# Sixteen sums of the convolution taps, from VectorE's adds to accumulating transfers on GpSimd's queue

## The chip, the core and the metric

The kernel runs on one core of a Trainium2 chip. TensorE multiplies matrices into PSUM, VectorE and ScalarE do the elementwise work, GpSimd does a little elementwise work and issues DMA transfers on its own queue, and SyncE issues the weight loads. The metric is the time of one execution in device microseconds; lower is better.

## The reference

One decoder layer with two token mixers in parallel, latent attention and a short gated convolution. The part that matters here is the convolution over 256 tokens and 2048 channels, with three taps:

```python
u = c_gate * c_in
u_pad = jnp.pad(u, ((0, 0), (CONV_K - 1, 0), (0, 0)))
conv = sum(conv_w[k] * u_pad[:, k:k + s] for k in range(CONV_K))
y_conv = jnp.einsum('bse,ed->bsd', b_gate * conv * jax.nn.silu(z_conv), w_o_conv)
```

For each token the result is `conv_w[2]*u[s] + conv_w[1]*u[s-1] + conv_w[0]*u[s-2]`. Around it stand the input projections (`h @ w_in`), the attention with 16 heads, the gates, and the output projections, all in float32.

## The kernel before

**Weights.** All weights come from HBM in units of 128 x 2048 numbers (1 MB), loaded by SyncE into three `raw` buffers. Each unit is split in two halves of 1024 columns. ScalarE copies a half to `whi` (the leading part of each number, line 245), and VectorE subtracts to get the rest, `wlo` (line 246). There are five buffers of each. A product of two such split matrices takes three matmuls. For one unit TensorE runs 24 matmuls, over two row blocks of 128 tokens (`t` = 0 and 1), and both halves are read in both row blocks. Every matmul is pinned in program order, and all have line 88.

**Heads and column blocks.** The middle of the kernel is a loop over 16 heads, `h = 4*v + at`. Beside the attention of head `h`, four units of `channels(h, i)` compute 512 columns of one of the four convolution projections. So four heads make one column block `j` of 512 channels: `u = c_gate * c_in` at `at` = 1, the gate `b_gate` at 2, `z_conv` at 3. `u` of block `j` and row block `t` is the tile `cv_f[:, j, t]` (128 tokens x 512 channels); the product of the gates is `cv_w[:, t]`.

**The taps.** `taps(j, t)` is a generator with three steps, resumed by hand with `next(tap)` between pieces of the attention:

- Step one. On GpSimd's queue, `u` is copied to two tiles shifted by one and two tokens (`mv1x`, `mv2x` in the code, `mv` in the profile, one buffer each); the first rows come from the earlier row block or from a memset. The rows of the convolution's weights for these taps are fetched, broadcast to 128 partitions (`cw`, two buffers).
- Step two. VectorE multiplies both shifted copies by their weights and adds the second to the first (line 785). The third tap's weights are fetched into a `cw` buffer that the first product has released.
- Step three. VectorE multiplies `u` by the third tap's weights and adds the sum of the other two to it (line 785).

After that `channels_join(j, t)` multiplies `u` by the gates (line 756), transposes it in 32 x 32 blocks into `cw` (t = 1) or `mv2x` (t = 0) on VectorE (line 320), and GpSimd's queue writes it to DRAM in four pieces (line 328, `far`) and brings it back turned (line 332). The joined blocks are split into `cv_both` (ScalarE and VectorE) in the next stage, at the second and third groups of projections.

For row block 1 the second step runs at `at` = 2 and the third at the end of that head, the join one head later. For row block 0 step one runs at the end of `at` = 3, steps two and three in the first four units of the next block's first head, and the join two units later. The last column block has no next block: its row block 0 follows directly on row block 1, and steps two and three run inside the last head.

**Order.** What is passed to `keep_in_program_order` is placed on its engine behind everything written before it; all taps, the transfers through DRAM and the softmax's transfers are pinned so. Weight splits, softmax arithmetic, the join's product and its transpose are placed by a planner, which fixes the order of each engine's queue when the kernel is built. An engine works its queue in that order, and a waiting instruction holds what stands behind it. GpSimd's queue carries all the transfers of the taps, of the softmax (`far<-via`, `p<-far`), of the gates (`far<-cw`, `at_f<-far`) and of the joins (`far<-mv`, `cv_f<-far`).

After the head loop the memory of `mv`, `cw` and the other temporaries is given up and used again by `at_both` and `cv_both`.

Of the kernel before, what the change touches and what calls it, by code (L numbers as in the profile page):

```python
# [15 lines left out]
ALU = mybir.AluOpType  # L16
# [66 lines left out]
def tile_layer(ctx: ExitStack, tc: tile.TileContext, xw, w0, xb, x, pos, pvec, post_g, wc, wz, wcv, wkr, wqk, wqr, wv, cwr, wsq, out):  # L83
    nc = tc.nc
# [223 lines left out]
    def temp(name, shape=(P, S), dt=F32, bufs=2, tag=None):  # L308

        tag, n = tag or name.rstrip("0123456789_"), shape[-1]  # L310
        if n % LINE == 0:
            return bp.tile(list(shape), dt, name=name, tag=tag, bufs=bufs)
        return bp.tile([P, -(-n // LINE) * LINE], dt, name=name, tag=tag, bufs=bufs)[:, :n]
# [449 lines left out]
    def taps(j, t):  # L763

        u, parts = cv_t[:, j, t, :], []

        def bring(dst, src):

            tc.keep_in_program_order(nc.gpsimd.dma_start(out=dst, in_=src))

        for d in (1, 2):
            m = temp(f"mv{d}", (P, 512), bufs=1, tag=f"mv{d}x")
            if t:
                bring(m[:d, :], cv_t[P - d :, j, 0, :])
            else:
                tc.keep_in_program_order(nc.gpsimd.memset(m[:d, :], 0.0))
            bring(m[d:, :], u[: P - d, :])
            parts.append(m[:, :])
        def tap(d):
            cw = temp("cw", (P, 512), bufs=2)  # L780
            bring(cw[:, :], cwr[2 - d : 3 - d, 512 * j : 512 * (j + 1)].to_broadcast([P, 512]))
            return cw

        def join(dst, a, b, op):
            tc.keep_in_program_order(nc.vector.tensor_tensor(dst, a, b, op=op))

        cws = [tap(d) for d in (1, 2)]
        yield
        for a, cw in zip(parts, cws):
            join(a, a, cw[:, :], ALU.mult)  # L790
        join(parts[0], parts[0], parts[1], ALU.add)
        cw = tap(0)
        yield
        join(u, u, cw[:, :], ALU.mult)
        join(u, u, parts[0], ALU.add)
        yield

    cv_w = bp.tile([P, NT, 512], F32, name="cv_w")
# [14 lines left out]
    for h in range(H):  # L813
# [88 lines left out]
        if at == 1:  # L902
            tap = taps(v, 1)
            next(tap)
        elif at == 3 and h + 1 < H or h == H - 2:
            tap = taps(v, 0)
            next(tap)
# [286 lines left out]
```

## Time and profile before

| | |
|---|---|
| median of 3 runs | 1035.13 us (1034.82 to 1035.21) |
| span of the profiled execution | 1033.7 us |
| TensorE busy | 1027.6 us, 99% |
| VectorE busy | 683.5 us, 66% |
| ScalarE busy | 527.4 us, 51% |
| GpSimd busy | 178.7 us, 17% |
| moved by DMA | 233.25 MB, 226 GB/s |

The page gives the span of the profiled execution, from its first to its last instruction; its own time is not listed beside it, and the three timed runs lie 1.1 to 1.5 us above the span. In the rows, PE is TensorE, PEld its weight loads, DVE VectorE, ACT ScalarE, POOL GpSimd and SP SyncE; L785 is line 785 of the kernel. A row of a group says how often an operation ran, its shortest, median and longest duration in ns, and the start of the first and the last in us. In a row of a timeline stand the start, the duration, the engine, the line and the operation; the bracket has the idle time before it and what ended it. In a row of DMA issues the last number is the median time from issue to landing.

### The profile page before, as it was taken

How to read it: one execution, taken by the hardware profiler on the slowest of the kernel's cores; microseconds unless marked ns; L12 is line 12 of the kernel's file. 1: busy time of each engine (PE TensorE's matmuls, PEld its weight loads, DVE VectorE, ACT ScalarE, POOL GpSimd, SP SyncE). 2: the span in 40 equal slices, each digit the busy share in tenths (PEclk: the TensorE clock that was granted, in tenths of full speed). 3: DMA queues.
4: the chain of work that ended last, by engine and by line, in shares of the span. 5: the costliest groups of instructions: out<-in, count | busy, mean ns of one | idle time of the engine just before them, and what ended most of it. 6: DMA issues, size and time to landing. Idle time of an engine off the chain costs nothing.

```text
span 1033.7 us, 12740 instructions
## 1 busy us (share of the span) xinstructions
PE 1027.6 (99%) x4684; PEld 856.7 (83%) x4684; DVE 683.5 (66%) x957; ACT 527.4 (51%) x735; POOL 178.7 (17%) x344
## 2 busy tenths in 40 slices
PE   9999999999999999999999999999999999999998
PEld 8888888888888888888888888888888888888886
DVE  7588787787777777777777785564455455455562
ACT  7665545655456454564555565344434444443451
POOL 4540421104300223112133120020010001002000
PEclk9999999999999999999999999999999999999999
DMA  9775865668665676857686765565565557558642
GB/s 353 278 261 204 276 221 219 211 197 288 215 250 193 223 265 209 275 187 242 228 270 226 265 217 199 204 226 185 200 219 209 188 201 241 183 188 337 228 163 81
DMA packets 44526, 233.25 MB, mean 226 GB/s; under 512 B 7952, under 2 KB 10512, under 8 KB 21552
## 3 DMA queue, kind: packets, MB, share of 16 engines
q1 hardware_dynamic: 32400, 199.67, 54.6%
q0 software_dynamic: 11632, 29.48, 8.8%
q10 hardware_dynamic: 432, 3.29, 0.8%
q8 instruction: 36, 0.59, 0.2%
q14 instruction: 26, 0.21, 0.1%
HBM read 215.66 MB, written 12.58 MB: 221 GB/s over the span
## 4 chain that ended last, share of the span: by engine, by line
PE 96%; DMA 2%; ACT 1%; DVE 0%; issue 0%; DVEq 0%; SPq 0%
PE cv L88 34%; PE sq L88 34%; PE out L88 8%; PE z L88 6%; PE qa L88 2%; PE vv L88 2%; PE kn L88 2%; PE qn L88 2%; PE ckv L88 2%; PE sc L88 1%; PE qr L88 1%; PE o L88 1%; DMA raw<-wz_dram 1%; DMA at_f<-far_qa 1%; DMA at_f<-far_ckv 0%
## 5 line engine op out<-in xcount | busy, mean ns | idle before, releaser
L246 DVE TENSOR_TENSOR wlo<-raw,whi 128x1024 fp32r<-128x1024 f32 (+1 forms) x370 | 440.5, 1196 | 279.8 <-ACT whi L245 268.4
L245 ACT ACTIVATE whi<-raw 128x1024 fp32r<-128x1024 f32 (+1 forms) x372 | 382.4, 1035 | 401.6 <-PE sq L88 180.5
L88 PE MATMUL cv<-whi,x_both 128*128 128x512 f32 x1024 | 319.8, 389 | 0.0
L88 PEld LDWEIGHTS cv<-whi,x_both 128*128 128x128 f32 x1024 | 192.3, 188 | 39.4
L88 PE MATMUL cv<-wlo,x_both 128*128 128x512 f32 x512 | 199.6, 390 | 0.0
L88 PE MATMUL sq<-whi,x_both 128*128 128x512 f32 x512 | 158.3, 389 | 0.0
L88 PEld LDWEIGHTS sq<-whi,x_both 128*128 128x128 f32 x512 | 96.1, 188 | 19.9
L88 PEld LDWEIGHTS cv<-wlo,x_both 128*128 128x128 f32 x512 | 96.1, 188 | 19.5 <-DVE wlo L246 0.2
L88 PE MATMUL sq<-wlo,x_both 128*128 128x512 f32 x256 | 99.6, 389 | 0.0
L88 PE MATMUL z<-whi,x_both 128*128 128x512 f32 x256 | 80.0, 389 | 0.0
L88 PE MATMUL sq<-whi,at_both 128*128 128x512 f32 x256 | 79.5, 389 | 0.0
L88 PE MATMUL sq<-whi,cv_both 128*128 128x512 f32 x256 | 79.5, 389 | 0.0
L88 PE MATMUL out<-whi,m_both 128*128 128x512 f32 x256 | 78.9, 389 | 0.0
L328 POOL DMA_DIRECT2D far<-sg x32 | 17.5, 553 | 313.0 <-DVE sg L320 238.4
L328 POOL DMA_DIRECT2D far<-via x64 | 35.1, 556 | 177.9 <-DVE via L320 177.9
L88 PEld LDWEIGHTS sq<-wlo,x_both 128*128 128x128 f32 x256 | 48.0, 188 | 10.0
L88 PEld LDWEIGHTS sq<-whi,at_both 128*128 128x128 f32 x256 | 48.0, 188 | 9.9
L88 PEld LDWEIGHTS out<-whi,m_both 128*128 128x128 f32 x256 | 48.0, 188 | 9.9
L88 PEld LDWEIGHTS sq<-whi,cv_both 128*128 128x128 f32 x256 | 48.0, 188 | 9.9
L88 PEld LDWEIGHTS z<-whi,x_both 128*128 128x128 f32 x256 | 48.1, 188 | 9.9
L88 PE MATMUL z<-wlo,x_both 128*128 128x512 f32 x128 | 49.8, 389 | 0.0
L88 PE MATMUL sq<-wlo,at_both 128*128 128x512 f32 x128 | 49.8, 389 | 0.0
(216 smaller groups left out, 1128.9 us busy)
## 6 DMA issues: line engine op xcount, KB each, us to landing
raw<-wsq_dram SPq DMA_DIRECT2D x80, 1024.0 KB, 4.8
raw<-wcv_dram SPq DMA_DIRECT2D x64, 1024.0 KB, 5.6
raw<-wz_dram SPq DMA_DIRECT2D x16, 1024.0 KB, 4.9
raw<-wqk_dram SPq DMA_DIRECT2D x8, 1024.0 KB, 6.0
cw<-cwr_dram POOLq DMA_DIRECT2D x24, 256.0 KB, 6.0
raw<-wc_dram SPq DMA_DIRECT2D x4, 1024.0 KB, 10.5
raw<-wv_dram SPq DMA_DIRECT2D x4, 1024.0 KB, 4.8
far<-via POOLq DMA_DIRECT2D x64, 48.0 KB, 4.1
```

Source lines behind the costliest of these rows:

```text
L88: return tc.keep_in_program_order(nc.tensor.matmul(*a, **kw))
L245: a = nc.scalar.activation(hi, src, AF.Copy)
L246: b = nc.vector.tensor_tensor(lo, src, hi.bitcast(F32), op=ALU.subtract)
L328: tc.keep_in_program_order(queue.dma_start(out=f[i], in_=m))
```

## The change

Both adds of `taps` become DMA transfers with an accumulating write: GpSimd's queue sends the one tile onto the other, and the transfer adds it. The first adds the second shifted product to the first; the second adds their sum to `u`. `taps` runs eight times (four column blocks, two row blocks), so sixteen adds of 128 x 512 float32 are replaced. The products stay on VectorE. The new transfers are pinned in program order on GpSimd's queue, the first ahead of the fetch of the third tap's weights.

```diff
+        def summed(dst, src):
+            tc.keep_in_program_order(nc.gpsimd.dma_start(out=dst, in_=src, accum_op=ALU.add))
+
         cws = [tap(d) for d in (1, 2)]
         yield
         for a, cw in zip(parts, cws):
             join(a, a, cw[:, :], ALU.mult)
-        join(parts[0], parts[0], parts[1], ALU.add)
+        summed(parts[0], parts[1])
         cw = tap(0)
         yield
         join(u, u, cw[:, :], ALU.mult)
-        join(u, u, parts[0], ALU.add)
+        summed(u, parts[0])
         yield
```

## The prediction

> **What bounds the kernel now.** I read the page first (busy shares, chain), then what TensorE waited for, then the chain in order of time. A row is start, duration and work, with the idle time before it in brackets.
>
> ```profile
> span 1033.7 us, 12740 instructions
> PE 1027.6 (99%) x4684; PEld 856.7 (83%) x4684; DVE 683.5 (66%) x957; ACT 527.4 (51%) x735; POOL 178.7 (17%) x344
> PE 96%; DMA 2%; ACT 1%; DVE 0%; issue 0%; DVEq 0%; SPq 0%
> ```
>
> The page's chain says that TensorE's own work makes up 96% of it. Its waits (us in total, times, longest), all rows that the view has for it, and then two pieces of the chain in order of time:
>
> ```profile
> PE idle L88 <- PEq L1182: 0.8, 1, 0.8
> PE fin L88 <- ACT dg L1069: 0.4, 1, 0.4
> PE vv L88 <- DVE f L396: 0.2, 1, 0.2
> 210.46 5.44 PE vv L88 x24
> 222.63 16.32 PE cv L88 x72
> ```
>
> TensorE is the bound. In the whole span it waited 1.4 us that the waits view can name (0.8 + 0.4 + 0.2), and only the 0.2 us was a wait for VectorE. The 72 matmuls in 16.32 us are three weight units of 24, so one unit of matmuls lasts 5.44 us. The matmul order is written out by hand, and the change leaves it alone. So the question is not what the sums cost VectorE, but whether a sum that lands later ever holds up a weight half that TensorE needs.
>
> Next, how busy the engines are where sums stand (the windows view: us, then TensorE, weight loads, VectorE, ScalarE, GpSimd, granted clock, DMA share, GB/s), and how far ahead of TensorE the splits work (timelines of ScalarE and VectorE).
>
> ```profile
> 210.00:262.00 52.00, 52.00 (x243) 43.48 (x242) 40.34 (x64) 27.43 (x41) 13.69 (x25) 1.00 0.71 240
> 600.16 1.06 ACT L245 ACTIVATE whi<-raw 128x1024 fp32r<-128x1024 f32 x1 [3.03 <-PE sq L88]
> 601.47 1.06 ACT L245 ACTIVATE whi<-raw 128x1024 fp32r<-128x1024 f32 x1 [0.24 <-PE sq L88]
> 601.26 2.53 DVE L246 TENSOR_TENSOR wlo<-raw,whi 128x1024 fp32r<-128x1024 f32 x2 [1.23 <-ACT whi L245]
> ```
>
> In the stretch around one sum VectorE works 40.34 of 52 us (78%), GpSimd 13.69, at a granted clock of 1.00. ScalarE's whi copies wait for TensorE to release one of five buffers: the split engines run at the end of their buffers. From this I estimate the cover. The release behind 600.16 comes when TensorE is through with the first half of its unit, 1.36 us (a quarter of 5.44) before that unit ends. That unit ends near 601.2 and the one after it at 606.6. At the release the buffers hold the other half of that unit, both halves of the next one and the first half of the one behind it; the freed buffer takes that last unit's second half. TensorE reaches it 1.36 us into the unit that starts at 606.6, at 608.0. Its wlo, the first of the two at 601.26, is ready at about 602.5. So VectorE may stand still for about 5.5 us before TensorE waits.
>
> **The change, part by part: what goes.**
>
> ```profile
> L785 DVE TENSOR_TENSOR mv<-mv,mv x8: 680/692/695, 151.3 to 582.3; 128x512 f32<-128x512 f32 x8
> L785 DVE TENSOR_TENSOR cv_f<-cv_f,mv x8: 678/687/693, 175.9 to 594.9; 128x512 f32<-128x512 f32 x8
> ```
>
> VectorE loses 8 x 0.692 + 8 x 0.687 = 11.0 us in sixteen pieces. TensorE's only wait for VectorE is 0.2 us, so this is worth between 0 and 0.2 us. I take 0.
>
> **What comes: sixteen transfers of 256 KB from SBUF to SBUF on GpSimd's queue.** No accumulating transfer is in the trace. Its nearest rows:
>
> ```profile
> L769 POOL DMA_DIRECT2D mv<-cv_f x24: 507/552/560, 138.7 to 573.4; - x24
> mv<-cv_f POOLq DMA_DIRECT2D x8, 254.0 KB, 4.2
> mv<-cv_f POOLq DMA_DIRECT2D x8, 252.0 KB, 5.2
> cw<-cwr_dram POOLq DMA_DIRECT2D x24, 256.0 KB, 6.0
> DMA to landing us min/median/max: 1.5/5.6/7.9
> cv_f<-x_dram SPq DMA_DIRECT2D x1, 2048.0 KB, 10.7
> ```
>
> An issue takes 0.55 us of GpSimd (below: 0.51, the shortest of that row; above, since two inputs are read: twice, 1.1), so 16 x 0.55 = 8.8 us (8.2 to 17.6) on an engine that is busy 17%. The landing, from issue: below 1.5 us, the fastest of line 769; above 10.7 us, the transfer of eight times the bytes. I take 6.0, the slow end of the plain 256 KB rows, because the accumulating one also reads its destination. DMA engines are 0.71 busy in this stretch; the data of sixteen sums, read twice and written once, are 16 x 0.75 = 12 MB, or 12 GB/s over the span beside the 240 of this stretch. I cost that at 0 because the whi copies wait for TensorE, not for weights.
>
> The Trainium skill gives, in "DMA: Bandwidth & Descriptors" (Anatomy of one DMA), a fit of about 2.0 us plus bytes over 436e3 for a DMA from GpSimd: an estimate of 2.6 us here. The plain rows above take 4.2 to 6.0, so the measurement decides; by the page the landing would be earlier and the sum stays 0.
>
> The Trainium skill also has a rule against this change, in "SBUF — State Buffer" (SBUF: two separate sides, the "DVE blocks DMA" trap): while VectorE runs a two-port operation, GpSimd cannot write the descriptors of its transfers. By it issues would stretch beside VectorE. The trace does not agree for these neighbours: 24 issues of line 769 lie between 0.507 and 0.560 us beside a VectorE that is busy most of the time.
>
> **Where the new waits stand.** A column block has a pair of sums for its second row block (t=1) and one for its first (t=0). For t=1, on VectorE, the second sum and its reader:
>
> ```profile
> 175.87 0.69 DVE L785 TENSOR_TENSOR cv_f<-cv_f,mv 128x512 f32<-128x512 f32 x1
> 198.26 0.69 DVE L756 TENSOR_TENSOR cv_f<-cv_f,cv_w 128x512 f32<-128x512 f32 x1
> ```
>
> and for t=0, rows of GpSimd and VectorE in order of time:
>
> ```profile
> 213.84 0.55 POOL L769 DMA_DIRECT2D cw<-cwr_dram  x1 [5.90 <-DVE mv L785]
> 215.37 0.69 DVE L785 TENSOR_TENSOR mv<-mv,mv 128x512 f32<-128x512 f32 x1
> 219.63 0.69 DVE L785 TENSOR_TENSOR cv_f<-cv_f,cw 128x512 f32<-128x512 f32 x1 [0.17 <-DMA cw<-cwr_dram]
> 223.49 1.22 DVE L246 TENSOR_TENSOR wlo<-raw,whi 128x1024 fp32r<-128x1024 f32 x1
> 224.62 0.68 DVE L756 TENSOR_TENSOR cv_f<-cv_f,cv_w 128x512 f32<-128x512 f32 x1
> 232.73 2.21 POOL L328 DMA_DIRECT2D far<-via  x4 [18.34 <-DVE via L320]
> 240.10 0.57 POOL L332 DMA_DIRECT2D p<-far  x1 [5.17 <-ACT whi L245]
> 255.69 2.17 POOL L328 DMA_DIRECT2D far<-mv  x4
> ```
>
> t=1: the second sum would come behind four far<-via issues of the softmax (2.21 us for four, as at 232.73 below), be issued near 178 and land near 184. Its reader, the join with cv_w (line 756), is at 198.3, 14 us later. Even at 10.7 us nothing waits. Cost 0, four times.
>
> t=0, first sum: it waits for both products (215.37), is issued by 215.9, and stands ahead of the tap-0 fetch, which moves from 213.84 to about 215.9, 2.1 us. That fetch would land near 222, so the product that reads it moves from 219.63 to about 222. If VectorE's order still has it ahead of the wlo at 223.49, the queue behind it (softmax sums, V splits, that wlo) stands about 2.4 us. That wlo now ends at 224.7 and is needed 5.44 + 1.36 us after the unit boundary at 222.63, at 229.4: cover 4.7 us. 2.4 is inside it.
>
> t=0, second sum: in GpSimd's program order it comes behind the four far<-via, so it moves from 221.7 on VectorE to an issue at 234.9 and lands near 241. Queued behind it on GpSimd are the softmax's return p<-far, which stands idle until 240.10 anyway, so the 0.55 us issue fits in its 5.17 us gap, and later far<-mv at 255.69, the first that reads the joined block. Join and transpose (0.68 + 0.70) then end near 243: 12 us of room. Cost 0, three times, as long as the join does not stand in VectorE's queue for more than 5.5 us.
>
> **The last block** is the tightest, since the next tap reuses the buffer that the second sum reads:
>
> ```profile
> 570.41 0.68 DVE L785 TENSOR_TENSOR cv_f<-cv_f,cw 128x512 f32<-128x512 f32 x1
> 571.88 0.52 POOL L776 MEMSET mv<- 1x512 f32 x1 [5.59 <-DVE cv_f L785]
> 581.00 1.31 DVE L785 TENSOR_TENSOR mv<-mv,cw 128x512 f32<-128x512 f32 x2 [0.20 <-DMA cw<-cwr_dram]
> 593.38 0.69 DVE L785 TENSOR_TENSOR cv_f<-cv_f,cw 128x512 f32<-128x512 f32 x1
> 597.59 0.68 DVE L756 TENSOR_TENSOR cv_f<-cv_f,cv_w 128x512 f32<-128x512 f32 x1
> 605.06 0.57 POOL L332 DMA_DIRECT2D cv_f<-far  x1 [0.58 <-DMA far<-mv]
> 607.87 4.26 ACT L245 ACTIVATE at_both<-at_f 128x512 fp32r<-128x512 f32 x8
> L88 PE MATMUL sq<-whi,at_both x256: 389/389/389, 633.9 to 916.6; 128*128 128x512 f32 x128
> 644.59 0.61 ACT L245 ACTIVATE cv_both<-cv_f 128x512 fp32r<-128x512 f32 x1
> ```
>
> With 6.0 us: the sum is issued at 571.1, lands at 577.1, so the memset is 5.2 us later and the two products start at 586.2 instead of 581.0. They end at 587.5; the first sum lands at 593.5; the fetch behind it is issued at 588.1 and lands at 594.1; the product runs to 594.8; the second sum lands at 600.8, and the join starts 3.2 us later than 597.59. The return to cv_f moves from 605.06 to about 608 and lands by 614. The split that reads it is at 644.59: 30 us of room. With 10.7 us everywhere the same chain gives a join at about 614 and a landing near 626, still 18 us early. The copies of at_both reuse memory that the last transposed transfer frees, so they move to about 609 (621 with 10.7, done by 626); TensorE first reads them at 633.9, so even this is inside. Sum over all parts: 0 us on TensorE's chain, 0 to 0.2 us gained. The profiled span of 1033.7 lies 1.4 us below the median of 1035.13, and I keep that distance: 1033.7 + 0 + 1.4 = 1035.1.
>
> **The rivals.** *First: the fetch is held by the sum ahead of it, and it is slower.* The tap-0 fetch stands right behind the first sum on one queue. If its data also waits for the sum's, it lands another 4 to 5 us later; with the 2.4 us above the product holds VectorE for 6.4 to 7.4 us against a cover of 4.7. Price 1.7 to 2.7 us in each of three blocks, and about as much again (4 x 1.5 us) where the last block waits at four points behind a landing later than its order expects: 3 x 2.2 + 6 = 12.6 us at most, 1041 in the middle. It decides once the fetch lands more than 8.3 us after its issue (6.0 + 4.7 - 2.4). For it: line 769 already reaches 7.9. Against it: the two mv<-cv_f transfers of a tap are issued close together on that queue and still land in 4.2 and 5.2 us. Chance 0.26.
>
> *Second: the accumulating transfer itself is slow.* Nothing in the trace bounds it firmly. Landing L us after issue against an order made for about 5.2, the t=0 join stands L - 5.2 us in VectorE's queue in four places, weight splits behind it; beyond 5.5 us of cover TensorE waits. It decides at L = 10.7; at 15 us it costs 4 x 4.3 = 17 us: 1052. The Trainium skill, "DMA: Bandwidth & Descriptors" (Rules for kernel authors), says that an accumulate reads its destination and writes it later; no run here shows what that costs. Chance 0.15; with a remainder of 0.02, slower has 0.43.
>
> *Third: a gain.* It needs TensorE to be waiting for VectorE. The waits name 1.4 us in all, the start included; less VectorE work cannot return more than 0.2 us unless the order of the splits falls out better. That also covers sums that turn out free. Time at best 1033. Chance 0.05.
>
> **How the numbers follow.** About 0.2%, 2 us, is what a measurement of this kernel can tell from no change. My forecast, everything hidden, has 0.52 and gives 1035.1. The range goes from 1033.4 (a little below the 0.2 us gain) to 1047 (the first rival's 12.6 us rounded down); it leaves out the second rival's 0.15 and what lies below. Alone, the likeliest case runs from 1034.5 to 1037.
>
> **What would show it.** Right: line 785 keeps 24 products and loses 16 sums, VectorE falls to about 672 us, GpSimd's rows gain sixteen issues near 0.55 us landing near 6, TensorE's waits stay under 2 us. Wrong: a row of TensorE waiting for wlo, near 220, 355, 489 or 585 to 610; VectorE waiting for cw (first rival) or for the sum at line 756 (second). A landing beyond 10.7 us breaks the forecast.

## The result, and the profile after

The changed kernel takes 1041.4 us in the median (1039.77 to 1041.79, three runs) against 1035.13 us: 1.0057 times as long, with a 95% interval of 1.0038 to 1.0077. The forecast of 1035.1 us with everything hidden was wrong; the time lies where the first rival put it, but that is luck, since the reason is another one. The profiled execution took 1039.77 us; its span is 1038.0 us, 4.3 us longer than before, and the two other runs were 1.6 and 2.0 us slower than it. Here and below, runs more than 1.5% above the fastest of their kernel are left out of the ratios; this concerns one run with plain copies and one with the fetches first.

The page of the changed kernel (span, busy time of each engine, shares of the chain), then all rows of TensorE's waits (us in total, times, longest):

```profile
span 1038.0 us, 12762 instructions
PE 1028.7 (99%) x4684; PEld 857.6 (83%) x4684; DVE 671.7 (65%) x941; ACT 528.6 (51%) x735; POOL 195.1 (19%) x360
PE 95%; DMA 2%; DVE 1%; issue 1%; POOL 0%; ACT 0%; DVEq 0%; ACTq 0%; POOLq 0%
PE o L88 <- DVE pt L246: 3.1, 1, 3.1
PE idle L88 <- PEq L1185: 0.8, 1, 0.8
PE fin L88 <- ACT dg L1072: 0.4, 1, 0.4
```

and the two longest rows of VectorE's waits that concern the taps:

```profile
DVE cv_f L756 <- DMA cv_f<-mv: 12.1, 4, 3.6
DVE mv L785 <- DMA cw<-cwr_dram: 9.5, 4, 7.3
```

VectorE lost 11.8 us of work and TensorE gained one wait of 3.1 us, in one place, for VectorE's split of `pt`: the softmax weights of a head, turned, which the `o` matmuls multiply with the values. Of VectorE's own two waits, which the rivals spoke of, the first is new, and the second was 4.1 us before; only a part of them reaches TensorE. Now the transfers: issues by line and tile (ns shortest/median/longest), then landings (us, median).

```profile
L788 POOL DMA_DIRECT2D mv<-mv x8: 896/920/980, 151.4 to 591.3; - x8
L788 POOL DMA_DIRECT2D cv_f<-mv x8: 867/956/974, 177.0 to 598.2; - x8
DMA to landing us min/median/max: 3.9/6.3/9.2
mv<-mv POOLq DMA_DIRECT2D x8, 256.0 KB, 5.5
cv_f<-mv POOLq DMA_DIRECT2D x8, 256.0 KB, 7.2
```

Landings of 5.5 and 7.2 us lie around the predicted 6.0. The first three blocks go as forecast in this execution. For the first block's t=0 (its second and third steps run beside the second block's first head) the rows of GpSimd and VectorE are:

```profile
214.62 0.90 POOL L788 DMA_DIRECT2D mv<-mv  x1 [7.71 <-DVE mv L785]
220.36 0.69 DVE L785 TENSOR_TENSOR cv_f<-cv_f,cw 128x512 f32<-128x512 f32 x1 [0.62 <-DMA cw<-cwr_dram]
231.52 0.97 POOL L788 DMA_DIRECT2D cv_f<-mv  x1
238.74 0.69 DVE L756 TENSOR_TENSOR cv_f<-cv_f,cv_w 128x512 f32<-128x512 f32 x1 [3.59 <-DMA cv_f<-mv]
```

The fetch behind the first sum holds its product for 0.62 us, not for 6. The join stands 3.59 us in VectorE's queue, less than the 5.5 us of cover, and TensorE shows no wait there.

The last block is where the time goes. Rows of VectorE, GpSimd and TensorE in order of time; the row that starts with 578.69 is a piece of the chain of waits, from the issue of the second weight fetch to the start of the product:

```profile
571.02 0.69 DVE L785 TENSOR_TENSOR cv_f<-cv_f,cw 128x512 f32<-128x512 f32 x1 [1.30 <-DMA cw<-cwr_dram]
572.01 0.88 POOL L788 DMA_DIRECT2D cv_f<-mv  x1 [6.81 <-DVE cv_f L785]
576.11 0.52 POOL L776 MEMSET mv<- 1x512 f32 x1 [2.66 <-DMA cv_f<-mv]
578.69 8.64 DMA cw<-cwr_dram
587.33 0.69 DVE L785 TENSOR_TENSOR mv<-mv,cw 128x512 f32<-128x512 f32 x1 [7.30 <-DMA cw<-cwr_dram]
589.07 0.69 DVE L785 TENSOR_TENSOR mv<-mv,cw 128x512 f32<-128x512 f32 x1
...
591.60 0.55 DVE L246 TENSOR_TENSOR pt<-p,pt 128x384 fp32r<-128x384 f32 x1
592.30 0.71 PE L88 MATMUL o<-pt,vv_hi 128*128 128x512 f32 x1 [3.15 <-DVE pt L246]
592.30 1.35 PE o L88 x4
593.65 349.26 PE sq L88 x1536
```

and of before, at the same place (not shown above):

```profile
573.90 1.10 POOL L769 DMA_DIRECT2D cw<-cwr_dram  x2
586.95 0.56 DVE L246 TENSOR_TENSOR pt<-p,pt 128x384 fp32r<-128x384 f32 x1
589.77 0.39 PE L88 MATMUL o<-pt,vv_hi 128*128 128x512 f32 x1
589.93 0.57 PE o L88 x4
590.51 348.20 PE sq L88 x1536
```

Up to here the changed execution runs 0.78 us ahead of the earlier one on TensorE, so rows of before are moved by that much below.

- The first product was late by 587.33 - (581.00 - 0.78) = 7.1 us. The product of `u` starts 571.02 - (570.41 - 0.78) = 1.4 us late, because its fetch stands behind the first sum and lands later. From that start to the memset it took 576.11 - 571.02 = 5.1 us instead of 571.88 - 570.41 = 1.5: 3.6 us for a transfer that landed in 4.05 us where VectorE added in 0.69. From the issue of the second weight fetch to the product it then took 8.64 us instead of 6.55 (before, that fetch was issued near 574.45, the middle of the row of two, and the product began at 581.00): 2.1 us of the 7.1. By their own landings the two fetches took 9.0 and 9.5 us, and 7.0 each before.
- The `pt` split stands in VectorE's queue behind both products, two `wlo` splits and two short operations of the attention. It starts 591.60 - (586.95 - 0.78) = 5.4 us late. Before, it was done at 587.51 for a matmul at 589.77: 2.3 us of cover. 5.4 - 2.3 = 3.1 us, the wait that TensorE shows.
- Then TensorE was slow. The four `o` matmuls and the matmuls of the next stage (`sq`) took 1.35 and 349.26 us; before, 0.57 and 348.20. That is 0.78 + 1.06 = 1.8 us on top of the wait, and the granted clock says why (windows of 1 us; the columns as in the windows row of before):

```profile
591.00:592.00 1.00, 0.00 (x0) 0.00 (x0) 0.97 (x3) 0.00 (x0) 0.70 (x2) 1.00 0.80 328
592.00:593.00 1.00, 0.70 (x2) 0.64 (x3) 0.97 (x3) 0.00 (x0) 0.75 (x2) 0.68 1.04 442
593.00:594.00 1.00, 1.00 (x6) 0.90 (x5) 1.00 (x2) 0.36 (x1) 0.00 (x0) 0.50 0.96 246
```

The clock is 1.00 during the wait, falls to 0.50 when TensorE works again, and comes back within the window of 595 (0.61 in the mean). Sum: -0.78 + 3.15 + 1.8 = 4.2 of the 4.3 us.

### The profile page after: what moved, and what is told of

Its sections match the earlier page's. It is cut to its first block, busy times and chain, and to the rows that moved or that the text cites. A ratio compares the mean times of both kernels' runs of the same rounds, so it can differ in the third digit from the quotient of the medians.

```text
span 1038.0 us, 12762 instructions
## 1 busy us (share of the span) xinstructions
PE 1028.7 (99%) x4684; PEld 857.6 (83%) x4684; DVE 671.7 (65%) x941; ACT 528.6 (51%) x735; POOL 195.1 (19%) x360
## 4 chain that ended last, share of the span: by engine, by line
PE 95%; DMA 2%; DVE 1%; issue 1%; POOL 0%; ACT 0%; DVEq 0%; ACTq 0%; POOLq 0%
PE sq L88 34%; PE cv L88 30%; PE z L88 8%; PE out L88 8%; PE qa L88 2%; PE kn L88 2%; PE qn L88 2%; PE vv L88 2%; PE ckv L88 2%; PE sc L88 1%; PE qr L88 1%; PE o L88 1%; DMA cw<-cwr_dram 1%; DMA mv<-mv 1%; DMA cv_f<-mv 0%
## 5 line engine op out<-in xcount | busy, mean ns | idle before, releaser
L245 ACT ACTIVATE whi<-raw 128x1024 fp32r<-128x1024 f32 (+1 forms) x372 | 382.9, 1035 | 401.1 <-PE sq L88 180.3
```

The costliest lines, as they stand in the source:

```text
L245: a = nc.scalar.activation(hi, src, AF.Copy)
```

## The experiments

Three theories stood against each other. **A**: one place costs, the second sum of the last block's t=1, through the `pt` split; the other fifteen transfers are nearly free. **B**: the loss is many small pieces, spread over all blocks. **C**: the accumulating write itself is slow, and a plain transfer would do no harm. Every kernel was timed beside the kernel before on the same chip; its medians there were 1035.17, 1035.69 and 1035.47 us for the three sets, and all 73 of its runs there had a mean granted clock of 0.999 or 1.000.

### All but the one sum, and only that one

```diff
-        summed(u, parts[0])
+        if (j, t) == (NV - 1, 1):
+            join(u, u, parts[0], ALU.add)
+        else:
+            summed(u, parts[0])
```

> All sums but one are transfers: the second sum of the last block's second row block (u plus the tap sum, near 572 us) is VectorE's add again. Theory A (the loss is one chain: that sum's landing holds the memset of the next tap, its copies and fetches, so the two products start 7 us late in VectorE's queue and the softmax split of head 15 behind them makes TensorE wait): the products start about 3.6 us earlier than in the changed kernel, TensorE's wait for pt falls from 3.1 us to 0 to 0.8 us, and the time is 1035 to 1036. Theory B (fifteen other transfers and issues of 0.9 us on GpSimd's queue, spread over the kernel, cost it): the time stays within 0.5 us of the changed kernel, near 1041.

Measured: 1036.26 us (1035.05 to 1038.64, 11 runs), ratio 1.0009 [1.0001, 1.0018]. Fifteen of sixteen transfers cost 0.1%, 0.3 us more than A's upper end. TensorE's wait for `pt` is gone.

The converse has this one transfer alone, all other sums on VectorE:

> Only that one sum is an accumulating transfer, the other fifteen are VectorE's. Theory A: the products start 3.6 to 5.7 us later than before, less a cover of 2.3 us that pt had, so TensorE waits 1.3 to 3.4 us for pt and, with the lower granted clock after the wait, the time is 1037 to 1040. Theory B: one sixteenth of the loss, 1035 to 1036.

Measured: 1036.48 us (1035.7 to 1040.33, 12 runs), ratio 1.0016 [1.0006, 1.0025]: between the two expectations. The profiled execution, the slowest, has the stall (`8.74` is the landing of the second weight fetch), while seven of the twelve runs lie below 1037:

```profile
PE o L88 <- DVE pt L246: 2.7, 1, 2.7
577.98 8.74 DMA cw<-cwr_dram
```

So the one transfer is enough to make the stall, but alone it does so only in some runs. In the changed kernel the chain starts 1.4 us later, behind the fetch that the first sum holds; here the first sum is an add, and the product of `u` starts without a wait. That this makes the difference is argued from the rows; no run has these two sums alone.

### Block by block

The last block's four sums alone as transfers:

> Only the last column block's four sums are transfers; the twelve of the first three blocks are adds on VectorE. Theory A (one place costs: in the last block the second sum of (3,1) delays the products, and behind them a pt split that TensorE has only 2.3 us of cover for; the other fifteen are nearly free): a wait of TensorE for pt of 2 to 3.5 us near 592, then a low granted clock, 1039 to 1041 us. Theory B (the loss is made of many small pieces in all four blocks): 1036 to 1037.

Measured: 1041.35 us (1037.08 to 1042.12, 6 runs), ratio 1.0047 [1.0031, 1.0063]. As much as the whole loss is in these four. The profiled execution took 1037.78 us and has the wait without the fall of the clock:

```profile
PE o L88 <- DVE pt L246: 2.2, 1, 2.2
```

Four of its six runs took 1041.3 to 1042.1 us at a mean granted clock of 0.996 or 0.997, and two 1037.1 and 1037.8 us at 0.999 and 1.000.

The complement, the twelve of the first three blocks:

> Twelve of the sixteen sums are transfers: those of the first three column blocks. The last block's four are VectorE's. Theory A (the loss comes from the last block alone, where the next tap follows at once and the memory is reused behind it): the time is that of the kernel before, 1035.2 within 0.5 us, and TensorE waits for no split. Theory B (issues and landings anywhere on GpSimd's queue): twelve sixteenths of the 6 us stay, 1039 to 1040.

Measured: 1036.96 us (1035.28 to 1039.91, 11 runs), ratio 1.0014 [1.0005, 1.0022]. Not nothing, as A had it, and not B's 4 us. Two landings of t=0 sums lay on its chain (the two pieces below), so the twelve were parted by row block:

```profile
232.47 7.54 DMA cv_f<-mv
368.31 7.11 DMA cv_f<-mv
```

> Only the t=0 pairs of the first three blocks are transfers (six). The kernel with twelve transfers there showed 1.3 to 1.4 us more than its comparison, and its chain of waits ran through the landing of cv_f<-mv that the t=0 join waits for at line 756 (7.1 to 7.5 us), with wlo splits behind it. If that wait is where those 1.3 us go: 1036.3 to 1037, and TensorE shows a wait of under 1 us. If they lie elsewhere (t=1, or GpSimd's extra issues): 1035.1 to 1035.9.

> Only the t=1 pairs of the first three blocks are transfers (six). Their second sum has 14 us until the join reads it. If the t=0 join is where the first three blocks lose: no difference, 1035.1 to 1035.9. If every transfer costs a little wherever it stands: about half of the 1.3 us, 1035.8 to 1036.5.

Measured: t=0 alone 1036.65 us (1035.15 to 1039.19, 12 runs), ratio 1.0012 [1.0003, 1.0020]; t=1 alone 1035.35 us (1034.54 to 1036.77, 11 runs), ratio 0.9998 [0.9989, 1.0006]. The t=1 transfers of these blocks are free, those of t=0 are not quite. TensorE's new wait in the t=0 kernel, and its rows around one join:

```profile
PE cv L88 <- ACT cv_f L743: 2.4, 3, 1.6
239.89 0.69 DVE L756 TENSOR_TENSOR cv_f<-cv_f,cv_w 128x512 f32<-128x512 f32 x1 [4.75 <-DMA cv_f<-mv]
247.13 0.42 DVE L463 TENSOR_TENSOR f<-rp_a,rp_b 128x256 f32<-128x256 f32 x1
247.59 0.86 ACT L245 ACTIVATE qr<-f 64x256 fp32r<-64x256 f32 x2 [1.91 <-DVE f L463]
248.47 0.69 ACT L743 ACTIVATE cv_f<-cv,r_both 128x512 f32<-128x512 f32 x1
249.21 0.50 PE L88 MATMUL cv<-whi,x_both 128*128 128x512 f32 x1 [0.55 <-ACT cv_f L743]
```

The join waits 4.75 us, inside the 5.5 us that the prediction had found for `wlo`. But the rotary arithmetic (`f`) is queued behind it too; ScalarE's split of `qr` waits for that, ScalarE's copy of `cv` out of PSUM stands behind the split, and TensorE needs that PSUM tile: 0.55 us here, 2.4 us over the three blocks.

The changed kernel once more, beside these three:

> The changed kernel once more, beside the three above on one chip. Theory A: 1040 to 1042, and equal to the last four alone plus 0 to 1.5 us. Theory B: 3 us or more above the last four alone.

Measured: 1039.24 us (1037.58 to 1043.83, 8 runs), ratio 1.0040 [1.0025, 1.0055]; below A's 1040 and below the last four alone. The intervals overlap, and the runs fall in the same two groups: five of 1037.6 to 1040.0 us at a granted clock of 0.999 or 1.000, three of 1041.1 to 1043.8 us at 0.996 or 0.997. So the median depends on which group had more runs. The profiled execution, the slowest, waited 3.9 us for `pt`.

### The transfer without the accumulation

```diff
-            tc.keep_in_program_order(nc.gpsimd.dma_start(out=dst, in_=src, accum_op=ALU.add))
+            tc.keep_in_program_order(nc.gpsimd.dma_start(out=dst, in_=src))
```

> All sixteen are plain copies of the same tiles instead of accumulating ones (the tap sums are left out of the computation, the order of every queue is the same). Theory A holds that a transfer with its landing stands where an add of 0.69 us stood: time within 2 us of the changed kernel, a wait for pt of 2 to 4 us. Theory C (the accumulating write is what is slow): issues fall from 0.92 to 0.55 us and landings from 5.5 and 7.2 us to 4 to 5 us, the wait for pt goes below 1 us, and the time to 1035 to 1037.

This kernel leaves the sums out of its result. Measured: 1037.7 us (1036.97 to 1039.65, 10 runs; an eleventh took 3703 us, for a reason that is not known), ratio 1.0024 [1.0015, 1.0033]: above what C gave and 3.7 us below the changed kernel, more than A allowed. Its rows (issue, landings, TensorE's wait):

```profile
L788 POOL DMA_DIRECT2D cv_f<-mv x8: 546/567/570, 176.8 to 596.6; - x8
mv<-mv POOLq DMA_DIRECT2D x8, 256.0 KB, 5.3
cv_f<-mv POOLq DMA_DIRECT2D x8, 256.0 KB, 5.8
PE o L88 <- DVE pt L246: 1.9, 1, 1.9
```

A plain copy lands in 5.3 and 5.8 us against 5.5 and 7.2 and makes a wait at the same place, of 1.9 us instead of 3.1. So C is not the whole cause: most of the loss comes of a transfer that stands where an add stood. The accumulation seems to add to it. With plain copies the product of `u` in the last block starts without a wait (at 569.43); in the four profiled kernels with an accumulating sum ahead of its fetch it waits for that fetch for 1.30 us (the changed one), 1.22 (all but one), 1.16 (last four) and 1.01 (the repeat). That is about the difference between the two stalls, though other pieces of the chain differ too. The times do not settle it: the interval here lies below the first one of the changed kernel (1.0038 to 1.0077), but overlaps the one beside the block runs.

### Moving the products behind the split

```diff
-        if at == 2 or h == H - 1:
+        if at == 2:
             next(tap)
-        if at == 2:
             arrive()
...
         if h == H - 1:
             pt = turn(ps_by_head.pop(h))
+            next(tap)
```

> All sixteen sums are transfers; in the last head the step with the two products comes after the softmax split of head 15 instead of before it, so that this split no longer stands behind the products on VectorE. Theory A: TensorE's wait for pt is gone, the granted clock stays at 1.00 near 590 to 600, the join of the last block is 2 to 5 us later but is read 40 us on: 1035 to 1036. Theory B: no change from the changed kernel, 1040 to 1042.

Measured: 1038.57 us (1038.24 to 1041.94, 6 runs), ratio 1.0038 [1.0026, 1.0051]; the 1035 to 1036 of A was missed. The wait for `pt` went and others came. TensorE's new waits, and ScalarE's copies of `at_both` here and in the changed kernel (there a view that ends behind the seventh of eight):

```profile
PE sq L88 <- ACT whi L245: 1.2, 1, 1.2
PE sq L88 <- DVE wlo L246: 0.8, 1, 0.8
614.80 4.28 ACT L245 ACTIVATE at_both<-at_f 128x512 fp32r<-128x512 f32 x8 [5.93 <-DMA far<-mv]
```

```profile
612.65 3.76 ACT L245 ACTIVATE at_both<-at_f 128x512 fp32r<-128x512 f32 x7 [0.48 <-DMA far<-mv]
```

The later chain of the last sums holds ScalarE for 5.93 us before `at_both`, with the `whi` copies behind it. Neither place of the products is free: the one is too late for the `pt` split, the other for `at_both`.

### Fetching the weights ahead of the copies

In `taps`, the two `cw` fetches stand ahead of the memsets and copies; in the second kernel the products are moved as well.

> All sixteen sums are transfers; the fetches of the first two weight rows are issued ahead of the memset and the shifted copies instead of behind them, so they no longer wait for the second sum's landing. The products then wait for the shifted copies alone, issued near 577. Theory A: in the last block the first product starts near 583 to 586 instead of 587.3, TensorE's wait for pt falls to 0.5 to 2.5 us: 1036.5 to 1039.5. Theory B: no change, 1041.

> All sixteen sums are transfers; fetches first and the last head's products behind the softmax split of head 15. The run with late products alone has shown a second wait in the last block: ScalarE stands at the copies of at_both until the last transposed transfer has released their memory, with weight copies queued behind. Theory A2 (both waits hang on the one late chain, which the earlier fetch shortens by 1 to 3 us): the wait for at_both falls from 5.9 to 3 to 5 us, TensorE's waits from 2.0 us to below 1 us, 1035.3 to 1037. Theory B: as with late products alone, 1038.6.

Measured: 1045.63 us (1036.44 to 1053.33, 8 runs), ratio 1.0088 [1.0058, 1.0118], and 1044.7 us (1039.13 to 1051.43, 6 runs), ratio 1.0092 [1.0066, 1.0118]. Both expectations were missed. The profiled execution of the first is its fastest, with a wait for `pt` of 1.1 us, and shows nothing that would explain 1053; its slower runs have granted clocks down to 0.994. What happens in them stays open.

### Work for TensorE in the gap

```diff
         if h == H - 1:
+            busy = bank("busy", tag="st", bufs=1)
+            for k in range(16):
+                matmul(busy[:, :], x_both[:, k, :P], x_both[:, k, :], start=k == 0, stop=k == 15)
             finish_all(values(h, pt))
```

> The changed kernel with sixteen more matmuls of 128x512, whose result is not used, right ahead of the products of head 15's softmax, 16 x 0.227 = 3.6 us of work where TensorE stood idle. If the granted clock falls because TensorE stood idle: the clock stays at 1.00 near 590 to 600, and the time is that of the kernel before plus the longer of 3.6 us and the wait, 1038.7 to 1040, below the changed kernel's 1041.4 although TensorE does more. If the low clock has another cause: 1041.4 to 1043.

Measured: 1040.3 us (1038.87 to 1040.99, 5 runs), ratio 1.0041 [1.0029, 1.0053], between the two expectations and nearer the first; granted clock 0.999 in every run, and 1.00 in every window of 1 us from 586 to 606. Where the stall was:

```profile
590.86 3.79 PE L88 MATMUL busy<-x_both 128*128 128x512 f32 x16
594.49 0.39 PE L88 MATMUL o<-pt,vv_hi 128*128 128x512 f32 x1
```

The `o` matmul starts 3.63 us behind the first of the extra ones and finds `pt` ready. TensorE did 3.6 us of useless work and the kernel was no slower than the changed one with a stall: the fall of the clock, and with it the group of runs above 1041 us, was gone in these five runs, where TensorE did not stand still. The median is 4.6 us above the kernel before, so 1.0 us is not accounted for by the extra matmuls.

## Why the prediction was wrong

**What held.** The sums' cost to VectorE and TensorE's indifference to it; the landings (6.0 predicted, 5.5 and 7.2 measured); t=1 of the first three blocks (0 predicted, ratio 0.9998). The first rival's mechanism, the fetch that is held by the sum ahead of it, is there but small: 0.62 us at t=0 and 1.30 us in the last block, where it makes 1.4 of the 7.1 us.

**The step that failed** is "The last block". It worked out that the two products start at 586.2 instead of 581.0, and then followed only what reads their result: the join, the return from DRAM, a split at 644.59 with 30 us of room. It did not ask what stands behind the products on VectorE. The rule used for t=0 (a waiting instruction holds its queue) was not applied here. Behind them come two `wlo` splits and the `pt` split of the last head, which before was ready only 2.3 us ahead of TensorE's need of it. Between the first product and that split the queue got 1.7 us shorter (7.1 us late became 5.4: the add of 0.7, a wait of 0.6 for `whi` and some spacing fell away). So the prediction's own 5.2 us would have given a stall of some 1.2 us (5.2 - 1.7 - 2.3); 3.15 was measured, with products 7.1 us late. The memset that waits for the sum, which starts it, was seen. Its delay came out right by luck (5.2 us predicted, 5.0 measured): the sum landed in 4.05 us and not in 6.0, but its product started 1.4 us late. The other 2.1 us are the slower weight fetch, which the prediction had left at its old time.

**Two smaller steps.** At t=0 the price of 0 was 1.2 us in the median: the cover of 5.5 us was that of `wlo`, while the rotary arithmetic in the same queue had less. And "even this is inside" for `at_both` followed TensorE's first use of it and not the `whi` copies behind it on ScalarE; in the changed kernel that wait is 0.48 us, and with later products it became 5.93.

**Two sizes.** The issue of an accumulating transfer reads 0.87 to 0.98 us instead of 0.55, on an engine with room for it; the issue behind it starts 0.56 to 0.61 us later all the same. The price of a stall was taken as its length; with the clock that follows it was 3.15 + 1.8 us.

**The rivals.** The first gave 1041 by fetch waits in three blocks and four waits in the last; nearly all of the loss is one wait in the last, with the lower clock behind it, which it had not placed. The second needed landings of the sums above 10.7 us; the longest was 9.2.

## What to carry to other kernels

When an instruction comes later, list what is queued behind it on its engine up to the next thing that the bounding engine reads, and take the smallest cover in that list; following the data alone finds room that is not there. A sum of 0.7 us that becomes a transfer of 4 to 9 us is free where nothing on that stretch of queue is due soon (here t=1 of the first blocks), and costly where a buffer's reuse hangs on it. Where the bounding engine is TensorE, a stall of two to four microseconds should be priced with the clock that can fall after it.

## What the runs showed of the hardware

**The clock after a short stall.** The stalls before the `o` matmul, and the granted clock behind them, in windows of 1 us: 1.93 us with plain copies, 2.18 us with the last four alone, and 3.94 us in the repeat. One row each:

```profile
593.00:594.00 1.00, 1.00 (x4) 0.81 (x3) 1.00 (x3) 1.00 (x2) 0.00 (x0) 0.50 0.73 275
```

```profile
593.00:594.00 1.00, 1.00 (x6) 0.82 (x5) 1.00 (x2) 0.85 (x2) 0.00 (x0) 1.00 0.91 203
```

```profile
599.00:600.00 1.00, 1.00 (x4) 0.81 (x3) 0.79 (x2) 0.00 (x0) 0.00 (x0) 0.50 0.84 336
```

In windows of 0.2 us, the clock was at 0.50 for 3.4 us after the stall of 1.93 us (591.8 to 595.2), and for 3.4 us after the 3.15 us of the changed kernel (592.4 to 595.8); after 2.18 us it did not fall; after 3.94 us it was at 0.50 for 6.8 us (594.0 to 600.9). So the length alone does not decide. In the 3.4 us ahead of a fall TensorE had stood still for 1.93, 3.15 and about 3.2 us of them; by this estimate from three executions, little more than half of such a stretch can be enough. The Trainium skill, "TensorE: Matmul & The Clock Gate" (Part 1: The HAM clock gate), puts the fall after an idle window of about 3.4 us, counted by windows that run on regardless of the kernel. The halved clock, the 3.4 us and the chance in it agree with the trace; a fall after 1.93 us is earlier than the page would have it, so the measurement decides.

**A fetch at a later place.** The weight fetches of 256 KB landed in 6.4 us in the median. The two in front of the last block's products landed in 7.0 us each before, where they were issued near 574; issued near 577 to 581, they took 9.0 and 9.5 us in the changed kernel, 8.4 and 9.1 with plain copies, 7.1 and 8.7 with the one transfer, and 7.5 to 7.7 with the last four. What they meet there was not tried, and it is not the worst place: a fetch issued at 285.58 in the changed kernel landed in 10.8 us, where nothing needed it soon.

**The issue of an accumulating transfer** is recorded with 0.87 to 0.98 us on GpSimd, a plain one between the same tiles with 0.55 to 0.57. The longer record does not hold the queue: the next issue starts 0.56 to 0.61 us behind an accumulating one, and a plain issue there reads 0.83 to 0.95 us itself.
